# Attention scores copied by ScalarE and masked in SBUF, four banks for one set of transposes, and scratch space turned into weight buffers, in a decoder layer on one core

## The chip, the core and the metric

The kernel runs on one core of one Trainium2 chip. The time is the device time of one execution in microseconds (us), and lower is better. The core has TensorE (PE in the profile), VectorE (DVE), ScalarE (ACT), GpSimd (POOL) and SyncE (SP), each with its own instruction queue that it works through in order, and DMA queues that move data between HBM and the on-chip buffer SBUF. TensorE writes into PSUM, of which this kernel uses eight banks of 128x512 fp32 words.

## The reference, cut to what matters

One layer with two branches over the same 256 tokens: causal attention with 8 heads of 128, and a gated unit that mixes positions within chunks of 128. All matrices are fp32. With 256 tokens there is only one attention block, so the gathering of past blocks falls away and attention is causal attention over 256 keys.

```python
D_MODEL = 2048; SEQ = 256; N_ATT_HEADS = 8; HEAD_DIM = 128

h = rms_norm(x, norm_g)
q, k, v, z_a, u_b, v_b, z_b, g_a, g_b = jnp.split(h @ w_in, cuts, axis=-1)
q = rms_norm(q.reshape(B, S, N_ATT_HEADS, HEAD_DIM), q_norm_g)
k = rms_norm(k.reshape(B, S, N_ATT_HEADS, HEAD_DIM), k_norm_g)
...
s_own = jnp.where(key_pos[None, :] <= q_pos[:, None], s_own, NEG_INF)
p = jax.nn.softmax(logits, axis=-1)
...
y_a = (att * jax.nn.silu(z_a)) @ w_proj_a
sgu = spatial_gating(jax.nn.gelu(u_b), jax.nn.gelu(v_b), sgu_norm_g, w_s, b_s)
y_b = (sgu * jax.nn.silu(z_b)) @ w_proj_b
merged = jax.nn.sigmoid(g_a) * y_a + jax.nn.sigmoid(g_b) * y_b
return x + merged @ w_out
```

## The kernel before

**The stream of weights.** `schedule()` cuts all the weight matrices into 120 pieces of 128x2048 fp32 words (1 MB each), numbered 0 to 119 in the order in which they are used: 8 pieces each ("quads") for q, k, v, za, vb, ub and zb, then four times 8 quads for the gates (g) and 4 pieces of the two branch projections (proj, results `y`), then two times 8 quads for the output (out). The main loop (`for i, ... in enumerate(G)`) loads piece i+3 (`load`, SyncE's queue), prepares piece i+2 (`split`) and multiplies piece i. The number at the end of a tile's name in the tables of order below is that of its piece: `wh28` belongs to piece 28, and za's quads are 24 to 31.

**fp32 from three multiplications.** A piece arrives as `raw`. ScalarE casts it to `wh` (L125), the high half; VectorE subtracts that from `raw` and gets `wl` (L126), the low half. The activations are cut the same way (`xuh`, `xul`), and each product is three matmuls (L288). In four or five of every 8 quads, seven block products take the place of eight: VectorE first forms sums of blocks in `t` (L143, L145, L146), and both `raw` and `t` are cut, into `whp` and `wlp` (L152, L155) and `th` and `tl` (L154, L157). Such a quad costs VectorE about three times a plain one.

**Buffers.** `raw` and `t` share the tag "raw" with 4 buffers; `wh` and `th` share "wh" with 3, `wl` and `tl` share "wl" with 3; "whp" and "wlp" have 2 each. A buffer is written again only when its last reader is done: a new `wh` waits until TensorE is through with the piece three back in that tag.

**Banks.** The main loop keeps two sets of four PSUM banks, E and L, that change places with each matrix. The quads of one matrix accumulate in L, those with seven products also in E; what happens beside them (transposes, scores, attention) uses the E banks before the first such quad needs them.

**Work around the change**, hung on pieces by `at(...)`:
- after quad 24: k is transposed (`ps_kT`); after quad 25, `score` makes six tiles of scores (two groups of four heads, three blocks of 128x128 per head) in the banks E[0..3], E[0], E[1]. Two lie below the diagonal and are copied by ScalarE (L424); four lie on it and VectorE copies their allowed part over tiles that GpSimd has filled with -1e30 (L410, L411, L426). `softmax` follows: row maximum (L432), exponentials with row sums (L437), reciprocals (L440).
- after quad 32 (vb's first): the probabilities are transposed; after quad 33, `attend` multiplies them with v into the four E banks (`ps_a`), and VectorE multiplies each bank into `za` (L464). Quad 34 is the first that needs the E banks again (`seven_vb`).
- after piece 64 (the first of proj 0): `turn_z` transposes `zb` into two banks, E[2] and E[3], each used twice; ScalarE casts to `zbh` (L490), VectorE makes `zbl` (L491). Pieces 66 and 67 multiply with these.

**Order.** For the first 8 quads ScalarE's and VectorE's order is that of the code. After it a scheduler places all instructions on all engines by priorities (the order in the code) and by its own estimate of when operands will be there, TensorE's matmuls among them.

Of the kernel before, what the change touches and what calls it, by code (L numbers as in the profile page):

```python
# [12 lines left out]
F32 = mybir.dt.float32  # L13
F32R = mybir.dt.float32r
# [3 lines left out]
ALU = mybir.AluOpType  # L18
AX = mybir.AxisListType

P = 128
# [5 lines left out]
NEG_INF = -1e30  # L27
ATT_SCALE = P ** -0.5
WORDS = 2048
B = 512  # L30
# [37 lines left out]
def hybrid_layer_kernel(  # L68
# [9 lines left out]
    nc = tc.nc  # L78
# [3 lines left out]
    const = ctx.enter_context(tc.tile_pool(name="const", bufs=1))  # L82
    big = ctx.enter_context(tc.tile_pool(name="big", bufs=10))
    unit = ctx.enter_context(tc.tile_pool(name="unit", bufs=10))
    wpool = ctx.enter_context(tc.tile_pool(name="wpool", bufs=6))
# [6 lines left out]
    def u(name, dtype=F32):  # L92
        return unit.tile([P, B], dtype, tag="u", name=name)
# [9 lines left out]
    raw, wh, wl, th, tl = {}, {}, {}, {}, {}  # L103

    def strassen(i):
        if i >= NG or G[i][0] != "quad" or G[i][1] == G[0][1]:
            return False
        return G[i][3] in SK or (G[i][1] == "g" and G[i][3] == 4)
# [2 lines left out]
        nc.sync.dma_start(raw[i][:, a:b], w[i, :, a:b])  # L111

    def new_raw(i):
        raw[i] = wpool.tile([P, WORDS], F32, tag="raw", bufs=4, name=f"raw{i}")

    def load(i, pieces=1):
        if i >= NG:
# [6 lines left out]
    def halve(h, l, r):  # L124
        nc.scalar.copy(h, r)  # L125
        nc.vector.tensor_tensor(l, r, f(h), op=ALU.subtract)  # L126

    def split(i, pieces=1, js=None):
        if i >= NG:
            return  # L130
        r = raw[i]
        if not strassen(i):
            if i not in wh:
                wh[i] = wpool.tile([P, WORDS], F32R, tag="wh", bufs=3, name=f"wh{i}")
                wl[i] = wpool.tile([P, WORDS], F32R, tag="wl", bufs=3, name=f"wl{i}")
            n = WORDS // pieces
            for j in js or range(pieces):
                sl = slice(j * n, (j + 1) * n)
                halve(wh[i][:, sl], wl[i][:, sl], r[:, sl])
            return  # L140
        t = wpool.tile([P, WORDS], F32, tag="raw", bufs=4, name=f"t{i}")
        two = t[:, 0:2 * B].rearrange("p (a n) -> p a n", a=2)
        nc.vector.tensor_tensor(two, r[:, B:3 * B].rearrange("p (a n) -> p a n", a=2),  # L143
                                r[:, None, 0:B].to_broadcast([P, 2, B]), op=ALU.add)
        nc.vector.tensor_tensor(t[:, 2 * B:3 * B], t[:, 0:B], r[:, 2 * B:3 * B], op=ALU.add)  # L145
        nc.vector.tensor_tensor(t[:, 3 * B:], t[:, 2 * B:3 * B], r[:, 3 * B:], op=ALU.add)  # L146
        wh[i] = wpool.tile([P, 3 * B], F32R, tag="whp", bufs=2, name=f"whp{i}")
        wl[i] = wpool.tile([P, 3 * B], F32R, tag="wlp", bufs=2, name=f"wlp{i}")
        th[i] = wpool.tile([P, WORDS], F32R, tag="wh", bufs=3, name=f"th{i}")
        tl[i] = wpool.tile([P, WORDS], F32R, tag="wl", bufs=3, name=f"tl{i}")  # L150
        a, b = slice(0, 2 * B), slice(2 * B, WORDS)
        nc.scalar.copy(wh[i], r[:, B:])  # L152
        for sl in (a, b):
            nc.scalar.copy(th[i][:, sl], t[:, sl])  # L154
        nc.vector.tensor_tensor(wl[i], r[:, B:], f(wh[i]), op=ALU.subtract)  # L155
        for sl in (a, b):
            nc.vector.tensor_tensor(tl[i][:, sl], t[:, sl], f(th[i][:, sl]), op=ALU.subtract)  # L157

    X = {}
# [45 lines left out]
    def split_x(kp, js=None):  # L205
        i, a = kp // 4, 2 * (kp % 4)
        for j in js or range(2):
# [8 lines left out]
    make_identity(nc, ident)  # L216
    mhalf = const.tile([P, 8], F32, name="mhalf")
    nc.gpsimd.memset(mhalf, -0.5)
    tri_f = u("tri_f").rearrange("p (h t) -> p h t", t=P)
    nc.gpsimd.memset(tri_f, 1.0)  # L220
    nc.gpsimd.affine_select(out=tri_f, in_=tri_f, pattern=[[0, 4], [-1, P]], base=0,
                            channel_multiplier=1, compare_op=ALU.is_ge, fill=0.0)
    tri = const.tile([P, 4, P], U8, name="tri")
    nc.gpsimd.tensor_copy(tri, tri_f)
    gain = const.tile([P, P], F32, name="gain")
# [180 lines left out]
    def score(banks):  # L406
        X["S1"] = slot(F32, "S1").rearrange("p (h t) -> p h t", t=S)
        for hg in range(2):
            X["S0", hg] = u(f"S0{hg}").rearrange("p (h t) -> p h t", t=P)
            nc.gpsimd.memset(X["S0", hg], NEG_INF)  # L410
        nc.gpsimd.memset(X["S1"][:, :, P:], NEG_INF)  # L411
        qT, kT = X["qT"], X["kT"]
        n = 0
        for hg in range(2):
            for c, b in ((0, 0), (1, 0), (1, 1)):
                ps = bank(banks[n % 4], f"ps_s{c}{hg}{b}")
                n += 1
                for h in range(4):
                    nc.tensor.matmul(ps[:, h * P:(h + 1) * P], qT[:, 4 * hg + h, c * P:(c + 1) * P],
                                     kT[:, 4 * hg + h, b * P:(b + 1) * P], start=True, stop=True)  # L420
                pv = ps.rearrange("p (h t) -> p h t", t=P)
                dst = X["S0", hg] if c == 0 else X["S1"][:, 4 * hg:4 * hg + 4, b * P:(b + 1) * P]
                if b < c:
                    nc.scalar.copy(dst, pv)  # L424
                else:
                    nc.vector.copy_predicated(dst, tri, pv)  # L426

    def softmax(hg):
        for c in range(2):
# [21 lines left out]
    def attend(hg, banks):  # L451
        v, pt = X["v"], X["PT", hg]
        for c in range(2):
            ps = bank(banks[c], f"ps_a{hg}{c}")
            for h in range(4):
                sl = slice(h * P, (h + 1) * P)
                nc.tensor.matmul(ps[:, sl], pt[:, c, h, :], v[0][hg][:, sl], start=True, stop=(c == 0))
                if c == 1:
                    nc.tensor.matmul(ps[:, sl], pt[:, 2, h, :], v[1][hg][:, sl], start=False, stop=True)
            za = X["za"][c][hg]  # L460
            for h in range(4):
                sl = slice(h * P, (h + 1) * P)
                nc.scalar.activation(za[:, sl], za[:, sl], AF.Copy, scale=X["rc", c, hg][:, h:h + 1])
            nc.vector.tensor_tensor(za, ps, za, op=ALU.mult)  # L464

    def mix(banks):
        for c in range(2):
# [170 lines left out]
    E, L = [0, 2, 4, 3], [1, 5, 6, 7]  # L638
    e = None
    for i, (kind, name, c, kp, n) in enumerate(G):  # L640
# [8 lines left out]
        if kind == "quad":  # L649
            if n == 0:  # L650
                if i and G[i - 1][0] == "quad":

                    E, L = L, E
# [39 lines left out]
        for fn, a in later.pop(i, []):  # L693
            a = list(a)
            if fn is sums:
                a[0] = X[a[1]]
            elif a and fn in (turn_qk, score, turn_p, attend, turn_z, mix, turn_m):
                if a[-1] is None:
                    a[-1] = list(E)
                    if fn is turn_p and a[0] == 1:  # L700
                        a[-1] = [E[3], E[0], E[1]]
                    if fn is attend:
                        a[-1] = E[2 * a[0]:]
                elif a[-1] == "late":
                    a[-1] = E[2:4]
                elif a[-1] == "L01":
                    a[-1] = L[0:2]
                elif a[-1] == "L23":
                    a[-1] = L[2:4]
                elif a[-1] == "L3":  # L710
                    a[-1] = L[3:4]
            fn(*a)
# [48 lines left out]
```

## Time and profile before

| | |
|---|---|
| three runs | 665.03, 666.70 and 666.89 us, median 666.7 us |
| the profiled execution | 664.48 us, of which its span 662.8 us |
| granted TensorE clock in the span | 1.000 |
| HBM read | 132.72 MB |

The span runs from the first to the last instruction. The profile's own slices (40 equal parts of the span, the busy share in tenths, 9 is 90% or more) show what kind of kernel this is:

```profile
PE   8999999999999999999999899999999999999997
DVE  4879898999999699999999999889989989998996
ACT  7889777757895678766656745655564556746460
POOL 1003003000020004000000000000000000000000
DMA  8975544634654534745457534935573573747651
```

TensorE is busy from end to end, VectorE nearly so, ScalarE two thirds, and the DMA engines half of the time after the first 30 us. A matmul's record is longer than the distance between two matmuls (they are pipelined), so a row of nines for PE doesn't say by itself that nothing is lost: that is read from the starts.

### The profile page before, as it was taken

Reading aid. Unit: us, or ns where it says so; the run is one execution under the profiler, and the core shown is the slowest. Engines: PE = TensorE matmul, PEld = TensorE weight load, DVE = VectorE, ACT = ScalarE, POOL = GpSimd, SP = SyncE. Lnnn points to the kernel's source line nnn. Section 1 sums busy time; section 2 is a strip of 40 time slices with the busy share of each in tenths; the row PEclk is TensorE's granted clock in tenths of the full one; section 3 lists DMA queues with packets and bytes.
Section 4 is the critical chain, followed back from the end, with each engine's and each line's share of the span. In section 5 each row is a group of like instructions: output and inputs, shape, how many; then the busy total and the mean of one; then the engine's idle time right before and its main releaser. Section 6 shows DMA issues by size and latency. Waiting matters only on the chain.

```text
span 662.8 us, 7853 instructions
## 1 busy us (share of the span) xinstructions
PE 652.3 (98%) x2980; PEld 538.4 (81%) x2980; DVE 606.6 (92%) x606; ACT 427.3 (64%) x560; POOL 27.2 (4%) x28
## 2 busy tenths in 40 slices
PE   8999999999999999999999899999999999999997
PEld 4888888888888888888888788888888888888886
DVE  4879898999999699999999999889989989998996
ACT  7889777757895678766656745655564556746460
POOL 1003003000020004000000000000000000000000
PEclk9999999999999999999999999999999999999999
DMA  8975544634654534745457534935573573747651
GB/s 308 417 294 191 200 181 151 252 122 176 247 170 154 224 128 164 280 136 209 163 190 283 182 139 158 351 156 181 206 296 112 182 278 142 254 163 282 201 180 63
DMA packets 22213, 135.32 MB, mean 204 GB/s; under 512 B 2464, under 2 KB 3104, under 8 KB 7072
## 3 DMA queue, kind: packets, MB, share of 16 engines
q1 hardware_dynamic: 21024, 132.73, 54.0%
q10 hardware_dynamic: 1152, 2.10, 1.0%
q8 instruction: 23, 0.38, 0.2%
q14 instruction: 14, 0.11, 0.0%
HBM read 132.72 MB, written 2.10 MB: 203 GB/s over the span
## 4 chain that ended last, share of the span: by engine, by line
PE 83%; DVE 8%; ACT 3%; DMA 2%; issue 2%; SPq 0%; DVEq 0%; ACTq 0%
PE acc_g L288 16%; PE y L288 13%; PE acc_out L288 9%; PE seven_g L288 8%; PE acc_q L288 6%; PE acc_ub L288 5%; PE acc_zb L288 5%; PE acc_k L288 5%; PE seven_out L288 3%; PE acc_vb L288 3%; DMA raw<-in_w 2%; PE acc_v L288 2%; DVE tl L157 2%; PE seven_zb L288 2%; PE seven_ub L288 2%
## 5 line engine op out<-in xcount | busy, mean ns | idle before, releaser
L126 DVE TENSOR_TENSOR wl<-raw,wh 128x2048 fp32r<-128x2048 f32 (+2 forms) x76 | 156.2, 2063 | 29.1 <-ACT wh L125 28.9
L154 ACT CAST th<-t 128x1024 fp32r<-128x1024 f32 x104 | 108.9, 1053 | 112.5 <-DVE t L143 50.2
L125 ACT CAST wh<-raw 128x2048 fp32r<-128x2048 f32 (+2 forms) x76 | 130.9, 1730 | 51.7 <-PE acc_g L288 17.1
L157 DVE TENSOR_TENSOR tl<-t,th 128x1024 fp32r<-128x1024 f32 x104 | 126.2, 1219 | 5.0 <-ACT th L154 4.7
L152 ACT CAST whp<-raw 128x1536 fp32r<-128x1536 f32 x52 | 76.6, 1481 | 31.1 <-DMA raw<-in_w 10.7
L155 DVE TENSOR_TENSOR wlp<-raw,whp 128x1536 fp32r<-128x1536 f32 x52 | 91.1, 1752 | 2.0 <-ACT whp L152 2.0
L143 DVE TENSOR_TENSOR t<-raw 128x1024 f32<-128x1024 f32 x52 | 63.4, 1219 | 1.1 <-DMA raw<-in_w 0.8
L288 PE MATMUL acc_g<-wh,xul 128*128 128x512 f32 x96 | 37.5, 390 | 1.8 <-ACT wh L125 1.8
L288 PE MATMUL acc_g<-wl,xuh 128*128 128x512 f32 x96 | 37.3, 389 | 0.0
L288 PE MATMUL acc_g<-wh,xuh 128*128 128x512 f32 x96 | 37.3, 389 | 0.0
L145 DVE TENSOR_TENSOR t<-t,raw 128x512 f32<-128x512 f32 x52 | 36.0, 691 | 0.2
L146 DVE TENSOR_TENSOR t<-t,raw 128x512 f32<-128x512 f32 x52 | 35.9, 691 | 0.2
L288 PE MATMUL acc_q<-wh,xuh 128*128 128x512 f32 x64 | 25.2, 393 | 1.3 <-ACT wh L125 1.3
L288 PE MATMUL acc_q<-wl,xuh 128*128 128x512 f32 x64 | 25.4, 396 | 0.4 <-DVE wl L126 0.4
L288 PE MATMUL y<-wh,zbl 128*128 128x512 f32 x64 | 25.1, 392 | 0.0
L288 PE MATMUL y<-wh,zah 128*128 128x512 f32 x64 | 25.0, 391 | 0.0
L288 PE MATMUL y<-wh,zal 128*128 128x512 f32 x64 | 25.0, 390 | 0.0
L288 PE MATMUL acc_q<-wh,xul 128*128 128x512 f32 x64 | 25.0, 390 | 0.0
L288 PE MATMUL y<-wl,zbh 128*128 128x512 f32 x64 | 24.9, 390 | 0.0
L288 PE MATMUL y<-wh,zbh 128*128 128x512 f32 x64 | 24.9, 390 | 0.0
L288 PE MATMUL y<-wl,zah 128*128 128x512 f32 x64 | 24.9, 389 | 0.0
L288 PE MATMUL acc_out<-wl,mh 128*128 128x512 f32 x64 | 24.9, 389 | 0.0
(497 smaller groups left out, 1586.3 us busy)
## 6 DMA issues: line engine op xcount, KB each, us to landing
raw<-in_w SPq DMA_DIRECT2D x116, 1024.0 KB, 4.9
raw<-in_w SPq DMA_DIRECT2D x7, 512.0 KB, 8.1
xnat<-in_x SPq DMA_DIRECT2D x2, 1024.0 KB, 12.7
xres<-in_x ACTq DMA_DIRECT2D x8, 256.0 KB, 4.5
out<-out_c SPq DMA_DIRECT2D x5, 256.0 KB, 2.5
xt<-in_xT SPq DMA_DIRECT2D x2, 512.0 KB, 8.4
xt<-in_xT SPq DMA_DIRECT2D x3, 256.0 KB, 9.0
raw<-in_w SPq DMA_DIRECT2D x2, 256.0 KB, 4.2
```

The source lines that it names most:

```text
L125: nc.scalar.copy(h, r)
L126: nc.vector.tensor_tensor(l, r, f(h), op=ALU.subtract)
L143: nc.vector.tensor_tensor(two, r[:, B:3 * B].rearrange("p (a n) -> p a n", a=2), r[:, None, 0:B].to_broadcast([P, 2, B]), op=ALU.add)
L145: nc.vector.tensor_tensor(t[:, 2 * B:3 * B], t[:, 0:B], r[:, 2 * B:3 * B], op=ALU.add)
L146: nc.vector.tensor_tensor(t[:, 3 * B:], t[:, 2 * B:3 * B], r[:, 3 * B:], op=ALU.add)
L152: nc.scalar.copy(wh[i], r[:, B:])
L154: nc.scalar.copy(th[i][:, sl], t[:, sl])
L155: nc.vector.tensor_tensor(wl[i], r[:, B:], f(wh[i]), op=ALU.subtract)
L157: nc.vector.tensor_tensor(tl[i][:, sl], t[:, sl], f(th[i][:, sl]), op=ALU.subtract)
L288: nc.tensor.matmul(acc, a, b, start=(start and n == 0), stop=(stop and n == 2))
```

## The change

- **Buffers:** "raw" gets 5 buffers in place of 4, "whp" 3 in place of 2. The space is taken from `dynamic_dma_scratch_size`, set to 1024 bytes.
- **Scores:** all six tiles are copied out of PSUM by ScalarE, whole; on the four diagonal ones VectorE then writes -1e30 above the diagonal, from a one-column constant `ninf` that is read broadcast. The mask `tri` is turned round for that (strictly above the diagonal). GpSimd's three fills of the score tiles go; one small fill for `ninf` comes.
- **attend:** its multiplication by `za` is given high priority in the scheduler.
- **turn_z for zb:** four banks, E[2], E[3], L[0], L[1], each used once. L[0] and L[1] hold gate 0's accumulators until VectorE has taken them out.

```diff
-        raw[i] = wpool.tile([P, WORDS], F32, tag="raw", bufs=4, name=f"raw{i}")
+        raw[i] = wpool.tile([P, WORDS], F32, tag="raw", bufs=5, name=f"raw{i}")
...
-        t = wpool.tile([P, WORDS], F32, tag="raw", bufs=4, name=f"t{i}")
+        t = wpool.tile([P, WORDS], F32, tag="raw", bufs=5, name=f"t{i}")
...
-        wh[i] = wpool.tile([P, 3 * B], F32R, tag="whp", bufs=2, name=f"whp{i}")
+        wh[i] = wpool.tile([P, 3 * B], F32R, tag="whp", bufs=3, name=f"whp{i}")
...
+    ninf = const.tile([P, 1], F32, name="ninf")
+    nc.gpsimd.memset(ninf, NEG_INF)
...
-    nc.gpsimd.affine_select(out=tri_f, in_=tri_f, pattern=[[0, 4], [-1, P]], base=0,
-                            channel_multiplier=1, compare_op=ALU.is_ge, fill=0.0)
+    nc.gpsimd.affine_select(out=tri_f, in_=tri_f, pattern=[[0, 4], [1, P]], base=0,
+                            channel_multiplier=-1, compare_op=ALU.is_gt, fill=0.0)
...
-            nc.gpsimd.memset(X["S0", hg], NEG_INF)
-        nc.gpsimd.memset(X["S1"][:, :, P:], NEG_INF)
...
-                if b < c:
-                    nc.scalar.copy(dst, pv)
-                else:
-                    nc.vector.copy_predicated(dst, tri, pv)
+                nc.scalar.copy(dst, pv)
+                if b == c:
+                    nc.vector.copy_predicated(dst, tri, ninf[:, None, :].to_broadcast([P, 4, P]))
...
-            nc.vector.tensor_tensor(za, ps, za, op=ALU.mult)
+            with tc.high_priority():
+                nc.vector.tensor_tensor(za, ps, za, op=ALU.mult)
...
                 elif a[-1] == "late":
-                    a[-1] = E[2:4]
+                    a[-1] = E[2:4] + L[0:2]
...
-    nc = bacc.Bacc("TRN2", target_bir_lowering=False, num_devices=1)
+    nc = bacc.Bacc("TRN2", target_bir_lowering=False, num_devices=1, dynamic_dma_scratch_size=1024)
```

The scheduler's placing moves on ScalarE and VectorE from the first seven-product quad to the end, since more buffers change its estimates. Three places matter.

**ScalarE around the scores.** Before, in its order (`wh`, `whp` and `th` are casts of weights, `S` are score tiles, `sm` row sums):

```order
L154 CAST th27_1258<-t27_1252 128x1024 x2
L125 CAST wh28_1334<-raw28_1250 128x2048
L424 COPY S1_1290<-ps_s100_1302 128x4x128
L424 COPY S1_1290<-ps_s110_1320 128x4x128
L152 CAST whp29_1413<-raw29_1332 128x1536
L437 ACTIVATE S00_1291,sm_1367<-S00_1291,nm_1365 128x128 x4
```

and with the change:

```order
L154 CAST th27_1260<-t27_1254 128x1024 x2
L152 CAST whp29_1416<-raw29_1335 128x1536
L125 CAST wh28_1337<-raw28_1252 128x2048
L423 COPY S00_1293<-ps_s000_1295 128x512
L423 COPY S1_1292<-ps_s100_1302 128x4x128
L423 COPY S1_1292<-ps_s101_1308 128x4x128
L423 COPY S01_1294<-ps_s010_1315 128x512
L423 COPY S1_1292<-ps_s110_1322 128x4x128
L423 COPY S1_1292<-ps_s111_1328 128x4x128
L436 ACTIVATE S00_1293,sm_1370<-S00_1293,nm_1368 128x128 x4
L152 CAST whp30_1453<-raw30_1410 128x1536
```

The six copies stand together behind `wh28`; `whp29` has moved ahead of them, and `whp30`, which stood behind all exponentials, stands between the first four of them and the rest.

**VectorE around attend.** Before (`ps_a` are the four results of attend, `t37` and `wl36` weights of later quads):

```order
L157 TENSOR_TENSOR tl35_1676<-t35_1669,th35_1675 128x1024 x2
L143 TENSOR_TENSOR t37_1788<-raw37_1755 128x1024
L464 TENSOR_TENSOR za0_c11_1538<-ps_a00_1707,za0_c11_1538 128x512
L145 TENSOR_TENSOR t37_1788<-t37_1788,raw37_1755 128x512
L464 TENSOR_TENSOR za0_h_1539<-ps_a01_1717,za0_h_1539 128x512
L464 TENSOR_TENSOR za0_c12_1541<-ps_a10_1731,za0_c12_1541 128x512
L126 TENSOR_TENSOR wl36_1758<-raw36_1667,wh36_1757 128x2048
L464 TENSOR_TENSOR za0_c22_1540<-ps_a11_1741,za0_c22_1540 128x512
```

and with the change:

```order
L143 TENSOR_TENSOR t37_1791<-raw37_1758 128x1024
L157 TENSOR_TENSOR tl35_1679<-t35_1672,th35_1678 128x1024 x2
L145 TENSOR_TENSOR t37_1791<-t37_1791,raw37_1758 128x512
L146 TENSOR_TENSOR t37_1791<-t37_1791,raw37_1758 128x512
L464 TENSOR_TENSOR za0_c11_1541<-ps_a00_1710,za0_c11_1541 128x512
L464 TENSOR_TENSOR za0_h_1542<-ps_a01_1720,za0_h_1542 128x512
L464 TENSOR_TENSOR za0_c12_1544<-ps_a10_1734,za0_c12_1544 128x512
L126 TENSOR_TENSOR wl36_1761<-raw36_1670,wh36_1760 128x2048
L464 TENSOR_TENSOR za0_c22_1543<-ps_a11_1744,za0_c22_1543 128x512
```

`t37` is out of the way of the first three products; `wl36` still stands between the third and the fourth.

**TensorE in proj 0.** Before, in the second half of piece 65 (`ps_zb` are the second two transposes of zb):

```order
L396 MATMUL ps_zb01_3039<-ident_113,zb0_c12_2643 128x128 x4
L396 MATMUL ps_zb11_3046<-ident_113,zb0_c22_2642 128x128 x4
L288 MATMUL y0_00_2997<-wh65_2955,zah_2011 128x512
L288 MATMUL y0_00_2997<-wl65_2956,zah_2011 128x512
L288 MATMUL y0_01_2998<-wh65_2955,zal_2012 128x512
L288 MATMUL y0_01_2998<-wh65_2955,zah_2011 128x512
L288 MATMUL y0_01_2998<-wl65_2956,zah_2011 128x512
L288 MATMUL acc_g1_0_3177<-wh68_3085,xul1_101 128x512
L288 MATMUL y2_00_3089<-wh66_2993,zbl_3024 128x512
```

and with the change all four transposes stand ahead of piece 65, and its end reads:

```order
L290 MATMUL y0_01_3001<-wh65_2958,zal_2015 128x512
L290 MATMUL y0_01_3001<-wh65_2958,zah_2014 128x512
L290 MATMUL y0_01_3001<-wl65_2959,zah_2014 128x512
L290 MATMUL y2_00_3092<-wh66_2996,zbl_3027 128x512
L290 MATMUL y2_00_3092<-wh66_2996,zbh_3026 128x512
L290 MATMUL y2_00_3092<-wl66_2997,zbh_3026 128x512
```

One matmul of quad 68 (`acc_g1_0`) stood between pieces 65 and 66; it now stands with the others of quad 68, behind piece 67. On SyncE's queue the small loads for the unit (`gain`, `ws`) stand behind six and two more weight loads than before. TensorE's instructions are the same in number and kind.

## The prediction

> **What bounds the kernel now.** I read the page's busy shares, the chain of waits, the list of TensorE's waits, a table of busy time by stage, and then the timeline of each wait.
>
> ```profile
> PE 652.3 (98%) x2980; PEld 538.4 (81%) x2980; DVE 606.6 (92%) x606; ACT 427.3 (64%) x560; POOL 27.2 (4%) x28
> ...
> 427.60 21.76 PE y L288 x96
> ```
>
> The lower line is a piece of the chain of waits, with start and length in us: 96 matmuls of 512 columns in 21.76 us, so TensorE starts one every 0.227 us when nothing holds it. The change takes away no matmul, so it can win only where the starts are further apart.
>
> ```profile
> engine line waited for: us in total, times, longest us
> PE acc_g L288 <- ACT wh L125: 1.8, 1, 1.8
> PE acc_q L288 <- ACT wh L125: 1.3, 1, 1.3
> PE ps_w L203 <- DVE warm L200: 1.3, 1, 1.3
> PE ps_s L419 <- DVE S L426: 1.1, 1, 1.1
> PE seven_vb L288 <- DVE za_c L464: 0.5, 1, 0.5
> ```
>
> These are TensorE's waits. `acc_q` and `ps_w` belong to the start, whose order on ScalarE and VectorE is written by hand and where the first loads are issued as before: nothing changes there. The other three are what the change touches: the scores (`ps_s`), attend (`seven_vb`), and proj 0 (`acc_g`).
>
> ```profile
> 134.90:184.20 49.30, 48.22 (x246) 40.88 (x245) 47.85 (x54) 34.01 (x57) 0.00 (x0) 1.00 0.46 171
> 184.20:234.20 50.00, 49.50 (x254) 41.64 (x253) 43.73 (x40) 33.40 (x44) 3.64 (x2) 1.00 0.50 179
> 234.20:276.80 42.60, 42.60 (x198) 35.49 (x197) 41.66 (x48) 35.31 (x73) 8.13 (x4) 1.00 0.54 198
> 276.80:321.20 44.40, 44.40 (x214) 37.37 (x213) 43.80 (x46) 30.44 (x40) 0.00 (x0) 1.00 0.52 189
> 321.20:387.40 66.20, 64.39 (x292) 52.80 (x291) 63.79 (x63) 40.30 (x37) 0.00 (x0) 1.00 0.53 192
> ```
>
> The stages za, vb, ub, zb, and gate 0 with proj 0: length, then busy time (and number) of PE, PEld, DVE, ACT and POOL, the granted clock, and DMA. VectorE is a close second: 47.85 of 49.30 us, 41.66 of 42.60, 43.80 of 44.40. So an earlier TensorE needs VectorE to be earlier too.
>
> **The scores.**
>
> ```profile
> 147.66 3.73 PE L419 MATMUL ps_s<-kT,qT 128*128 128x128 f32 x32
> 149.36 2.42 DVE L157 TENSOR_TENSOR tl<-t,th 128x1024 fp32r<-128x1024 f32 x2
> 150.43 1.89 ACT L125 CAST wh<-raw 128x2048 fp32r<-128x2048 f32 x1
> 151.70 0.72 DVE L426 COPY_PREDICATED S<-tri,ps_s 128x512 f32<-128x512 uint8 x1
> 152.47 2.05 PE L419 MATMUL ps_s<-kT,qT 128*128 128x128 f32 x16 [1.08 <-DVE S L426]
> ...
> 367.09 0.87 PE ps_zb L396 x8
> ```
>
> Eight short matmuls take 0.87 us (last line, from the chain), 0.109 each. The first 32 fill four banks and would let the next start at 147.66 + 32 x 0.109 = 151.15; it starts at 152.47, **1.3 us** late, because VectorE is at `tl` until 151.70 and only then empties the first bank.
>
> With the change ScalarE empties it. Its six copies stand behind `wh28`, which needs the buffer that TensorE gives up with quad 25, at 147.7. In the trace this cast ran only from 150.43, since it stood behind a `th` that waited for VectorE; with a fifth `raw` buffer VectorE forms that `t` earlier.
>
> ```profile
> L424 ACT COPY S<-ps_s 128x512 f32<-128x512 f32 x2 | 1.2, 582 | 0.9 <-PE ps_s L419 0.9
> L154 ACT CAST th<-t 128x1024 fp32r<-128x1024 f32 x104 | 108.9, 1053 | 112.5 <-DVE t L143 50.2
> L152 ACT CAST whp<-raw 128x1536 fp32r<-128x1536 f32 x52 | 76.6, 1481 | 31.1 <-DMA raw<-in_w 10.7
> ```
>
> Walk ScalarE's new order with these lengths. Back from 147.66, quad 25 takes 24 x 0.227 = 5.4 us and k's 16 transposes 1.7 ahead of it, so the first of these is complete at 140.9. Four evictions like L424's end at 143.2, two `th` at 145.2, `whp29` at 146.6; `wh28` can run from 147.7 to 149.6. The first bank is then free at 150.2, 0.9 us before it is needed, the second at 150.8. I take the whole 1.3 us as gone; the bounds are 0 (`wh28` as late as in the row, copies from 152.3) and 1.3.
>
> ```profile
> L426 DVE COPY_PREDICATED S<-tri,ps_s 128x512 f32<-128x512 uint8 x4 | 2.8, 730 | 0.0
> L145 DVE TENSOR_TENSOR t<-t,raw 128x512 f32<-128x512 f32 x52 | 36.0, 691 | 0.2
> ```
>
> ScalarE gets four copies more, 4 x 0.58 = 2.3 us; it is busy 34.01 of 49.30 us in this stage, and that idle time hides them. VectorE keeps four masked copies, now with SBUF on both sides. The trace shows no such one: between 0.69 us, what 512 fp32 words take from SBUF alone (L145), and 0.73 as now, that is 0 to 0.16 us less in all. I take 0.
>
> [...]
>
> The change also adds a wait. `whp30` now stands between the first exponentials and the others, and its buffer (the third in that tag) is `whp26`'s, free when TensorE ends quad 26.
>
> ```profile
> 167.52 2.36 DVE L157 TENSOR_TENSOR tl<-t,th 128x1024 fp32r<-128x1024 f32 x2 [0.39 <-ACT th L154]
> L437 ACT ACTIVATE S<-S,nm 128x128 f32<-128x128 f32 (+1 forms) x16 | 7.0, 440 | 1.5 <-DVE nm L434 1.5
> ```
>
> Without the stall the scores end at 147.66 + 48 x 0.109 = 152.9, and quad 26 at 152.9 + 21 x 0.227 = 157.7. Behind `whp30` (1.4 us) wait twelve of the sixteen exponentials (5.6 us, counting these wider), then the two halves of `th29`, and VectorE's `tl29` waits for those: 164.7, 166.7, 168. In the trace `tl29` ended at 169.88 (the first row), 1.9 us later, while TensorE is only 1.3 us earlier. So this wait costs nothing.
>
> **Attend.**
>
> ```profile
> 200.09 1.89 ACT L125 CAST wh<-raw 128x2048 fp32r<-128x2048 f32 x1
> 203.55 2.28 DVE L126 TENSOR_TENSOR wl<-raw,wh 128x2048 fp32r<-128x2048 f32 x1
> 205.75 0.68 DVE L464 TENSOR_TENSOR za_c<-ps_a,za_c 128x512 f32<-128x512 f32 x1
> ...
> 205.59 0.39 PE L288 MATMUL seven_vb<-th,Flx 128*128 128x512 f32 x1
> 206.49 0.50 PE L288 MATMUL seven_vb<-th,Flx 128*128 128x512 f32 x1 [0.50 <-DVE za_c L464]
> ```
>
> TensorE loses 206.49 - 205.59 - 0.23 = 0.67 us, waiting for the fourth product, which stands behind `wl36`. High priority doesn't lift it over `wl36`, as the order shows; it takes `t37` (0.69, L145) out from between the others. VectorE came to `wl36` at 203.55, when `wh36` had been ready since 201.98, so the fourth product can come 0.7 to 1.6 us earlier, if ScalarE keeps pace. Against it, fourteen scalings of `za` now stand on ScalarE between the last probabilities' evictions and `wh36`, where eight stood. Bounds: 0 and 0.67 us won; I take **0.5**.
>
> **Proj 0.**
>
> ```profile
> 374.09 0.39 PE L288 MATMUL y<-wl,zah 128*128 128x512 f32 x1
> 376.29 0.50 PE L288 MATMUL acc_g<-wh,xul 128*128 128x512 f32 x1 [1.81 <-ACT wh L125]
> ...
> 374.33 1.90 ACT L125 CAST wh<-raw 128x2048 fp32r<-128x2048 f32 x1 [0.41 <-PE y L288]
> ```
>
> 376.29 - 374.09 - 0.23 = **2.0 us** lost, and it had to be lost in that order. The one matmul of quad 68 needs `wh68`; its buffer is `wh65`'s, which TensorE gives up with the last matmul of piece 65, the one just before. So ScalarE could cast only while TensorE stood still. In the new order this matmul stands behind piece 67, 48 x 0.227 = 10.9 us later. What is late next?
>
> ```profile
> 366.72 1.28 DVE L346 TENSOR_TENSOR g_c<-acc_g,g_c 128x512 f32<-128x512 f32 x2
> 371.31 1.28 DVE L491 TENSOR_TENSOR zbl<-ps_zb,zbh 128x512 fp32r<-128x512 f32 x2
> ```
>
> The two new banks are free when VectorE has read gate 0's first two accumulators, here at 367.4 and 368.0. With all transposes from 367.09 on, the third and fourth ask at 368.0 and 368.4: no stall, with 0.4 us to spare. Piece 66 starts at 367.09 + 16 x 0.109 + 24 x 0.227 = 374.3 and reads only the first two tiles of `zbl`, which were there at 372.6; with `t69` put ahead of them (1.2 us) it is 373.8. I take 2.0, with 1.0 (VectorE a us later) and 2.0 as bounds.
>
> **The buffers** cost no time of their own. What they win is seen where ScalarE waits for loads.
>
> ```profile
> 357.36 1.92 ACT L125 CAST wh<-raw 128x2048 fp32r<-128x2048 f32 x1 [2.38 <-DMA raw<-in_w]
> ```
>
> A load is issued when a buffer comes free and lands 4.9 us later (the page's median), so one buffer more starts it some us earlier. TensorE didn't wait for this cast, so I count nothing; it is the slack on which the terms above rest. GpSimd's three fills go, and nothing in TensorE's list waited for GpSimd. `gain` and `ws` come six and two loads later on SyncE's queue and are used two stages on.
>
> **The sum:** 1.3 + 0.5 + 2.0 = 3.8 us. The profiled execution took 664.48 us (span 662.8 and 1.7 around it): 660.7. The median of the runs, 666.7, lies 2.2 above that execution, so I forecast 666.7 - 3.8 = **662.9 us** for a median.
>
> **The rivals.**
>
> ```profile
> 113.13 0.39 PE L288 MATMUL seven_v<-th,Fhx 128*128 128x512 f32 x1
> 113.54 0.50 PE L288 MATMUL seven_v<-tl,Fhx 128*128 128x512 f32 x1
> ```
>
> - *All small waits go too.* Here 0.41 - 0.23 = 0.18 us is lost; I found four such places, some 0.8 us. With these and 0.2 more at attend: 4.8, 661.9 us.
> - *ScalarE takes VectorE's place at the scores.* If `wh28` ends after 150.6 the first copy ends after 151.2, and each us beyond is lost again; at the row's 152.3 all of it: 666.7 - 2.5 = 664.2. For it: the cast stands ahead of the copies, as before. Against: it waited for a `t` that comes earlier now.
> - *VectorE becomes the bound.* It is busy 98% from 234 to 321, so what is won at the scores and at attend may be lost again before 360; proj 0's 2.0 stays: 664.7. For it: the table. Against: in stage vb it is idle 6.3 of 50.0 us, where it can catch up.
> - *Slower: casts to the third `whp` buffer block ScalarE.* In most stages a `whp` cast now stands ahead of a `wh` cast (`whp35` ahead of `wh33`). Its load needs a `raw` buffer that VectorE frees with `wl31`, about 173 by my walk; it lands near 178, and ScalarE's queue stands still till then. `wl33` is made at 183.5 and TensorE asks for it at 191 (quads 31 and 32 and the transposes after 177.5). It decides where a load lands more than those 7 us later; at 0.6 us in each of ten stages it is 6.0 lost against 3.8 won: 668.9.
> - *Nothing is won:* all three waits come back as others, 666.7.
>
> **Chances.** Forecast 0.56, small waits too 0.09, ScalarE 0.10, VectorE 0.15, nothing 0.05, slower 0.05. A measurement here can tell about 0.3%, 2.0 us, from no change. The forecast, the larger gain and most of ScalarE's case lie beyond it, and under half of VectorE's: 0.78 faster, 0.17 within, 0.05 slower. The range takes the sum's bounds (4.8 to 1.0 us won, 661.9 to 665.7) and, below, the runs' own spread (665.03 is 1.7 under the median): 660.2 to 665.9.
>
> **What would show it.** Right: in TensorE's waits `ps_s` from `S` and `acc_g` from `wh` are gone; `seven_vb` is under 0.3 us; the first score copy starts before 151. Wrong: `ps_s` waits for ScalarE; TensorE waits for `wl` or `tl` between 230 and 360 (VectorE the bound); ScalarE idle ahead of `whp` for loads with TensorE waiting behind it.

## The result and the profile after

| | before | changed |
|---|---|---|
| median of 6 runs each | 666.24 us (664.47 to 666.89) | 660.78 us (660.26 to 662.89) |
| ratio | 1 | 0.993, 95% interval 0.9917 to 0.9943 |
| the profiled execution | 664.48 us, span 662.8 | 660.26 us, span 658.5 |

The changed kernel is faster by 5.5 us in the medians and by 4.2 us between the two profiled executions. The busy times on its page:

```profile
PE 650.4 (99%) x2980; PEld 538.7 (82%) x2980; DVE 606.3 (92%) x606; ACT 427.8 (65%) x564; POOL 25.3 (4%) x26
```

TensorE, VectorE and ScalarE have as much to do as before; GpSimd, without its fills, has 1.9 us less. The list of TensorE's waits (what waited for what; us in total, times, longest):

```profile
PE acc_v L290 <- DVE wl L126: 1.3, 1, 1.3
PE ps_w L203 <- DVE warm L200: 1.3, 1, 1.3
PE acc_q L290 <- ACT wh L125: 1.2, 1, 1.2
PE acc_q L290 <- DVE wl L126: 0.2, 1, 0.2
```

The three waits of the prediction (`ps_s`, `seven_vb`, `acc_g`) are gone, and one has come that it didn't see: `acc_v` waits 1.3 us for a low half. The scores in the changed kernel's timeline (start, length, engine, line, operation):

```profile
147.07 1.06 ACT L154 CAST th<-t 128x1024 fp32r<-128x1024 f32 x1 [1.78 <-DVE t L146]
148.03 1.47 ACT L152 CAST whp<-raw 128x1536 fp32r<-128x1536 f32 x1
148.50 5.52 PE L419 MATMUL ps_s<-kT,qT 128*128 128x128 f32 x48
149.40 1.90 ACT L125 CAST wh<-raw 128x2048 fp32r<-128x2048 f32 x1
151.20 2.54 ACT L423 COPY S<-ps_s 128x512 f32<-128x512 f32 x5
151.69 2.28 DVE L126 TENSOR_TENSOR wl<-raw,wh 128x2048 fp32r<-128x2048 f32 x1
153.89 2.13 DVE L425 COPY_PREDICATED_SCALAR S<-tri,ninf 128x512 f32 x3
```

All 48 score matmuls run in one piece. The first copy, though, starts at 151.20; the fifth group of matmuls asks for its bank at 148.50 + 32 x 0.109 = 151.99, so the copy (0.58) is in time by 0.2 us; the prediction's mark, a first copy before 151, is missed by as much. The new wait, in VectorE's, GpSimd's and TensorE's rows:

```profile
109.57 1.38 POOL L244 TENSOR_TENSOR rs<-ms,mhalf 128x4 f32<-128x4 f32 x1 [0.41 <-DVE ms L243]
110.98 0.23 DVE L369 TENSOR_SCALAR rs<-rs,rstd 128x4 f32<-128x4 f32 x1 [0.90 <-POOL rs L244]
111.12 0.68 DVE L146 TENSOR_TENSOR t<-t,raw 128x512 f32<-128x512 f32 x1
111.72 1.75 DVE L155 TENSOR_TENSOR wlp<-raw,whp 128x1536 fp32r<-128x1536 f32 x1
113.39 2.28 DVE L126 TENSOR_TENSOR wl<-raw,wh 128x2048 fp32r<-128x2048 f32 x1
...
114.02 0.39 PE L290 MATMUL acc_v<-wh,xuh 128*128 128x512 f32 x1
115.73 0.51 PE L290 MATMUL acc_v<-wl,xuh 128*128 128x512 f32 x1 [1.32 <-DVE wl L126]
```

VectorE waits for GpSimd's power (`pow`, in k's normalization), then finishes `t21`, makes `wlp21`, and only then `wl20`, which TensorE needs first. Before, `wl20` started at 110.07, straight behind the last of k's four small multiplies:

```profile
109.93 1.83 DVE L367 TENSOR_SCALAR rs<-rs,rstd 128x4 f32<-128x4 f32 x1 [0.75 <-POOL rs L242]
110.07 2.29 DVE L126 TENSOR_TENSOR wl<-raw,wh 128x2048 fp32r<-128x2048 f32 x1
```

So the waits for GpSimd were there before; what is new is `t21` and `wlp21` ahead of `wl20`. With a fifth `raw` buffer `t21` has somewhere to go, so the scheduler puts piece 21's sums ahead of `wl20` (e5 and e6 below bear this out). TensorE loses 115.73 - 114.02 - 0.23 = 1.48 us.

**A balance.** For every kernel I took the distances between the starts of all consecutive matmuls, less 0.227 us (0.2267 unrounded; 512 columns) or 0.109 us (128), and added up by place what is left: TensorE's lost time in us. The places are times of the profiled execution: the start, v's and k's stretch (80 to 140 us), the scores (140 to 160), the attention with its transposes (180 to 220), proj 0 (360 to 400).

| | median us | start | 80-140 | scores | attention | proj 0 | rest | behind the start |
|---|---|---|---|---|---|---|---|---|
| before | 666.24 | 4.7 | 0.35 | 1.54 | 1.32 | 2.32 | 0.76 | 6.29 |
| changed | 660.78 | 4.2 | 1.68 | 0.16 | 0.38 | 0.02 | 0.34 | 2.58 |
| e1 scores' edit alone | 666.84 | 4.9 | 0.42 | 2.09 | 1.39 | 2.15 | 0.80 | 6.85 |
| e2 banks alone | 662.58 | 5.0 | 0.25 | 1.64 | 1.35 | 0.02 | 0.75 | 4.01 |
| e3 both buffers alone | 660.57 | 5.4 | 0.60 | 0.16 | 0.39 | 0.08 | 0.36 | 1.59 |
| e4 priority alone | 665.48 | 5.4 | 0.02 | 1.64 | 1.26 | 3.94 | 0.76 | 7.62 |
| e5 `raw` buffer alone | 663.05 | 4.6 | 1.92 | 1.41 | 0.90 | 0.08 | 0.37 | 4.68 |
| e6 `whp` buffer alone | 663.43 | 4.5 | 2.73 | 1.88 | 1.31 | 0.13 | 0.77 | 6.82 |
| e7 changed, no buffers | 663.52 | 5.4 | 0.25 | 2.15 | 1.50 | 0.05 | 0.75 | 4.70 |
| e9 buffers, multiplies on GpSimd | 659.56 | 4.6 | 0.05 | 0.16 | 0.40 | 0.08 | 0.38 | 1.07 |
| e10 changed once more | 660.46 | 4.5 | 1.44 | 0.16 | 0.41 | 0.02 | 0.33 | 2.36 |
| e11 changed, multiplies on GpSimd | 659.73 | 5.9 | 0.03 | 0.16 | 0.40 | 0.02 | 0.33 | 0.94 |

The first two rows: 1.4 us came from the scores, 0.9 from the attention, 2.3 from proj 0, 0.4 from small waits and 0.5 from the start; 1.3 went to the new wait. That is 4.2, as between the profiled executions. The start differs by up to 1.7 us among kernels whose first 8 quads are the same, so its part is not the change's.

### The profile page after: what moved, and what is told of

It reads as the page before. It is cut to its first block, busy times and chain, and to the rows that moved or that the text cites. A ratio compares the mean times of both kernels' runs of the same rounds, so it can differ in the third digit from the quotient of the medians.

```text
span 658.5 us, 7820 instructions
## 1 busy us (share of the span) xinstructions
PE 650.4 (99%) x2980; PEld 538.7 (82%) x2980; DVE 606.3 (92%) x606; ACT 427.8 (65%) x564; POOL 25.3 (4%) x26
## 4 chain that ended last, share of the span: by engine, by line
PE 93%; DVE 3%; POOL 1%; DMA 1%; issue 1%; ACT 0%; SPq 0%; DVEq 0%
PE acc_g L290 16%; PE y L290 13%; PE acc_out L290 9%; PE seven_g L290 8%; PE acc_q L290 6%; PE acc_vb L290 5%; PE acc_za L290 5%; PE acc_ub L290 5%; PE acc_zb L290 5%; PE acc_k L290 4%; PE seven_out L290 3%; PE acc_v L290 2%; PE seven_vb L290 2%; PE seven_zb L290 2%; PE seven_ub L290 2%; PE seven_za L290 2%
## 5 line engine op out<-in xcount | busy, mean ns | idle before, releaser
L290 PE MATMUL acc_out<-wh,mh 128*128 128x512 f32 x64 | 24.9, 389 | 0.0
```

The costliest lines, as they stand in the source:

```text
L290: nc.tensor.matmul(acc, a, b, start=(start and n == 0), stop=(stop and n == 2))
```

## The experiments

The theory under test is the prediction's: each wait is undone by its own edit. The rival: what counts is the order that the buffers bring.

### One part of the change alone

**e1, the scores' edit alone.** The kernel before with

```diff
+    ninf = const.tile([P, 1], F32, name="ninf")
+    nc.gpsimd.memset(ninf, NEG_INF)
...
-                if b < c:
-                    nc.scalar.copy(dst, pv)
-                else:
-                    nc.vector.copy_predicated(dst, tri, pv)
+                nc.scalar.copy(dst, pv)
+                if b == c:
+                    nc.vector.copy_predicated(dst, tri, ninf[:, None, :].to_broadcast([P, 4, P]))
```

(with the turned mask, the fills left out and the smaller scratch).

> The kernel before with the scores' edit alone (copy on ScalarE, mask written in SBUF; the descriptor scratch is cut too, since the constant needs room, but no buffer is added). Theory (each wait is undone by its own edit): TensorE's 1.25 us loss at the scores goes and nothing else, so the span of 662.8 us falls by 1.1 to 1.4 us, and the losses at the attention products (0.67 us) and at the projection (1.97 us) stay. Rival (what changed is the order that the buffers bring): without the buffers ScalarE's copies come too late, the loss at the scores stays over 0.6 us and the span falls by less than 0.7 us.

Measured: 666.84 us against 665.99 us of the kernel before; ratio 1.0011, interval 0.9998 to 1.0024. Nothing is won. From e1's list of TensorE's waits, and from ScalarE's timeline:

```profile
PE ps_s L419 <- ACT S L423: 1.6, 1, 1.6
```

```profile
150.84 1.89 ACT L125 CAST wh<-raw 128x2048 fp32r<-128x2048 f32 x1
152.64 2.53 ACT L423 COPY S<-ps_s 128x512 f32<-128x512 f32 x5
```

TensorE now waits for ScalarE's copy, which stands behind `wh28`, and `wh28` is as late as it was before. The wait has changed its owner and grown from 1.25 to 1.80 us. That is the prediction's rival "ScalarE takes VectorE's place", in a kernel without the buffers. e1 also has the changed kernel's smaller scratch, and the balance shows no loss of before reduced by more than 0.2 us: the scratch by itself isn't what wins in the runs with more buffers.

**e2, the four banks alone.**

```diff
-                    a[-1] = E[2:4]
+                    a[-1] = E[2:4] + L[0:2]
```

> The kernel before with four banks for the transposes of the spatial product alone. Theory: the misplaced wait of 1.8 us for a weight half at 374 us goes, and the span falls by 1.8 to 2.2 us; the other losses stay. Rival: the loss at 374 us was the late weight half itself, which the buffers bring earlier; with the banks alone at least 1 us of it stays.

Measured: 662.58 us against 665.99; ratio 0.995, interval 0.9938 to 0.9963. All of proj 0's loss goes and nothing else; the span falls by 2.0 us, to 660.8, as the theory said. TensorE's waits of e2 that are left behind the start:

```profile
PE ps_s L419 <- DVE S L426: 1.2, 1, 1.2
PE seven_vb L288 <- DVE za_c L464: 0.6, 1, 0.6
```

The median fell by 3.4, more than the span; the last section comes back to that.

**e3, both buffers alone.**

```diff
-        raw[i] = wpool.tile([P, WORDS], F32, tag="raw", bufs=4, name=f"raw{i}")
+        raw[i] = wpool.tile([P, WORDS], F32, tag="raw", bufs=5, name=f"raw{i}")
...
-        wh[i] = wpool.tile([P, 3 * B], F32R, tag="whp", bufs=2, name=f"whp{i}")
+        wh[i] = wpool.tile([P, 3 * B], F32R, tag="whp", bufs=3, name=f"whp{i}")
```

(`t` too gets 5, and the scratch is cut).

> The kernel before with the buffers alone (five raw buffers, three for the products' high halves, scratch cut). Theory: the three named losses stay (1.25, 0.67 and 1.97 us), the new wait of 1.3 us for VectorE's low half at 114 us comes in by this edit alone, and about 1.2 us of small losses (at 12 us, 182 us, 577 us) go, so the span moves by less than 0.6 us to either side. Rival: the buffers do most of the work, the loss at 374 us falls below 1 us, and the span falls by more than 1.5 us.

Measured: 660.57 us against 665.99; ratio 0.9917, interval 0.9904 to 0.9931. This is the changed kernel's whole gain. The theory said that the span would hardly move, and fell here. The one wait of TensorE behind the start, and the scores in the timeline:

```profile
PE acc_v L288 <- DVE wl L126: 0.3, 1, 0.3
```

```profile
148.63 5.52 PE L419 MATMUL ps_s<-kT,qT 128*128 128x128 f32 x48
150.99 0.73 DVE L426 COPY_PREDICATED S<-tri,ps_s 128x512 f32<-128x512 uint8 x1
```

The wait for `wl20` comes by this edit, though shorter than in the changed kernel (the last section says why).

VectorE still empties the first bank, as before the change, at 150.99 (before: 151.70) and in time: the bank is wanted at 148.63 + 3.5 = 152.1. Here TensorE also comes later (148.63, before 147.66), since its start lost more; e9 below shows the same without that help. At the attention `wl36` starts at 202.01 (before: 203.55), the fourth product is done at 204.89, and TensorE goes on without a stop:

```profile
202.01 2.28 DVE L126 TENSOR_TENSOR wl<-raw,wh 128x2048 fp32r<-128x2048 f32 x1
204.21 0.68 DVE L464 TENSOR_TENSOR za_c<-ps_a,za_c 128x512 f32<-128x512 f32 x1
204.98 0.47 PE L288 MATMUL seven_vb<-th,Flx 128*128 128x512 f32 x1
```

**e4, the priority alone.**

```diff
-            nc.vector.tensor_tensor(za, ps, za, op=ALU.mult)
+            with tc.high_priority():
+                nc.vector.tensor_tensor(za, ps, za, op=ALU.mult)
```

> The kernel before with the priority of the attention's last multiply alone. Theory: the loss of 0.67 us at 205 us falls to about 0.1 us and the span by 0.4 to 0.7 us. Rival: the multiply waits for ScalarE's scaling of za and not for its place on VectorE, so the priority alone changes the loss by less than 0.2 us.

Measured: 665.48 us against 665.99; ratio 0.9998, interval 0.9987 to 1.001. From e4's timeline:

```profile
203.98 2.28 DVE L126 TENSOR_TENSOR wl<-raw,wh 128x2048 fp32r<-128x2048 f32 x1
206.18 0.68 DVE L465 TENSOR_TENSOR za_c<-ps_a,za_c 128x512 f32<-128x512 f32 x1
...
206.91 0.50 PE L288 MATMUL seven_vb<-th,Flx 128*128 128x512 f32 x1 [0.68 <-DVE za_c L465]
```

`wl36` stands ahead of the fourth product, and VectorE's and ScalarE's whole order is that of before, instruction by instruction. TensorE loses 0.84 us at this place instead of 0.67. The loss didn't fall, so the theory is wrong; the reason that the rival gave (ScalarE's scaling) is wrong too, since the product stands behind `wl36`.

### Which buffer

**e5, five `raw` buffers alone; e6, three `whp` buffers alone** (each with the smaller scratch).

```diff
-        raw[i] = wpool.tile([P, WORDS], F32, tag="raw", bufs=4, name=f"raw{i}")
+        raw[i] = wpool.tile([P, WORDS], F32, tag="raw", bufs=5, name=f"raw{i}")
```

> The kernel before with the fifth raw buffer alone (and the scratch cut that makes room for it). Theory (the raw buffer lets VectorE form the sums of a later piece while it would idle, so they no longer stand behind the scores and the attention): the losses at the scores and at 374 us go (under 0.3 us each), that at the attention falls, the wait for a low half at 114 us comes in, and the span ends within 1 us of that with all buffers (658.8 us). Rival (the third high-half buffer is what counts): the loss at the scores stays over 1 us and the span over 661 us.

```diff
-        wh[i] = wpool.tile([P, 3 * B], F32R, tag="whp", bufs=2, name=f"whp{i}")
+        wh[i] = wpool.tile([P, 3 * B], F32R, tag="whp", bufs=3, name=f"whp{i}")
```

> The kernel before with the third high-half buffer alone. Theory (raw buffer): the loss at the scores stays as it was (1.25 us), that at the attention does not fall (0.67 us or more), only the misplaced wait at 374 us goes, span about 660.8 us as with the banks alone, median about 662.6 us. Rival (the high-half buffer counts): all three go, span under 659.5 us.

Measured: 663.05 and 663.43 us against 665.89 us; ratios 0.9957 (0.9945 to 0.997) and 0.9965 (0.9952 to 0.9978). Both expectations failed in part: proj 0 is mended by either buffer alone, the scores by neither (1.41 and 1.88 us lost). In e5 the wait for `wl20` came as expected (0.98 us); e6, whose span I put at 660.8 us, took 663.0 in the profiled execution, the slowest of its five (the others: 661.5 to 661.8), and got a wait of its own there:

```profile
PE seven_v L288 <- DVE tl L157: 1.5, 1, 1.5
```

How far VectorE gets by the scores shows why one buffer doesn't do. The window from 30 to 148 us in the kernel before (length, then busy time of PE, PEld, DVE, ACT, POOL):

```profile
30.00:148.00 118.00, 117.98 (x539) 97.91 (x538) 105.81 (x109) 88.88 (x156) 12.98 (x12) 1.00 0.53 205
```

and with the `raw` buffer alone (e5):

```profile
30.00:148.00 118.00, 116.71 (x531) 96.43 (x530) 106.50 (x111) 89.59 (x157) 13.98 (x12) 1.00 0.59 221
```

with the `whp` buffer alone (e6):

```profile
30.00:148.00 118.00, 115.89 (x527) 95.78 (x526) 103.07 (x107) 87.95 (x155) 12.99 (x12) 1.00 0.53 204
```

and with both (e3):

```profile
30.00:148.00 118.00, 117.70 (x536) 97.62 (x536) 108.60 (x112) 91.08 (x159) 15.92 (x12) 1.00 0.59 221
```

VectorE has the same work in all four. By 148 us it has done 105.81 us of it before, 106.50 with the `raw` buffer, 103.07 with the `whp` buffer, and 108.60 with both. So with both it is 2.8 us further when the scores come; with one alone the gain is 0.7 us or none. With `raw` alone a sum can be formed early, but its casts still wait for a `whp` buffer; with `whp` alone there is no early `t` to cast: so I read it, and no run takes that apart further.

At 114 us the two runs show what each buffer moves. In e5 the last of piece 21's sums (112.64) stands ahead of `wl20` (113.24), and `wlp21` behind it (115.44). In e6 `wl20` starts at 112.21, straight behind the multiplies as before the change, and the sums follow. `t21` ahead of `wl20` is the fifth `raw` buffer's doing; `wlp21` came ahead as well only with both.

### The change without its buffers

**e7**: the changed kernel with `raw` back at 4 and `whp` at 2; scores' edit, priority and banks stay.

```diff
-        raw[i] = wpool.tile([P, WORDS], F32, tag="raw", bufs=5, name=f"raw{i}")
+        raw[i] = wpool.tile([P, WORDS], F32, tag="raw", bufs=4, name=f"raw{i}")
...
-        wh[i] = wpool.tile([P, 3 * B], F32R, tag="whp", bufs=3, name=f"whp{i}")
+        wh[i] = wpool.tile([P, 3 * B], F32R, tag="whp", bufs=2, name=f"whp{i}")
```

> The changed kernel with the buffers taken back (four raw buffers, two for the high halves); the scores' edit, the priority and the four banks stay. Theory (the buffers carry the scores and the attention, the banks only the projection): TensorE loses about 1.8 us at the scores, waiting for ScalarE's copy, and about 0.8 us at the attention, nothing at 374 us; median 662.3 to 663.3 us. Rival (the edits work together and need no buffers): median under 661.3 us.

Measured: 663.52 us against 665.89; ratio 0.9962, interval 0.9949 to 0.9976. 0.2 us over the theory's bounds and 2.2 over the rival's. The scores lose as in e1, the banks win what they win alone. TensorE's waits behind the start:

```profile
PE ps_s L419 <- ACT S L423: 1.7, 1, 1.7
...
PE ps_p L447 <- ACT PT L448: 0.4, 1, 0.4
PE seven_vb L290 <- DVE za_c L464: 0.3, 1, 0.3
```

At the attention the loss is spread over two waits now (0.53 and 0.45 us by the starts).

### The new wait

**e8 and e11**: the changed kernel with k's four small multiplies on GpSimd, behind its powers, so that VectorE waits for none of them.

```diff
-                    nc.vector.tensor_scalar(rs, rs, scale, None, op0=ALU.mult)
+                    nc.gpsimd.tensor_scalar(rs, rs, scale, None, op0=ALU.mult)
```

> The changed kernel with k's four small multiplies (rs by rstd) moved from VectorE to GpSimd, so that VectorE does not wait for GpSimd's powers ahead of the low half of piece 20. Theory: the four waits of 0.75 to 0.90 us on VectorE go, the low half is ready about 3 us sooner, the wait of 1.3 us at 114 us goes, and the span falls by 0.5 to 1.5 us (the wait takes up what the start of an execution varies by, so between executions less than 1.48 us). Rival: what stands ahead is the sums of piece 21 and not the waits, so the wait at 114 us stays over 0.8 us and the time does not change; or the longer round on GpSimd delays k's scaling and TensorE waits at k's transposes.

Measured: 659.92 us against 665.89; ratio 0.9915, interval 0.9899 to 0.9931. TensorE's wait for `acc_v` is gone. Its profiled execution was the slowest of its five (662.09 us, span 660.4) and lost 7.2 us at the start, more than any other, so its span tells nothing, and the balance has e11, the same kernel, in its place. To set it beside the changed kernel on one chip, both ran again:

> The changed kernel as it is, beside the other two on one chip. Both theories: 660.3 to 661.0 us median, the wait at 114 us there again (0.3 to 1.4 us, the longer the sooner TensorE got away at the start); it is the measure for the two others.

> The changed kernel with the four small multiplies on GpSimd once more, beside the changed kernel. Theory: 0.5 to 1.2 us faster than the changed kernel in the medians, no wait at 114 us. Rival (the difference to the changed kernel was one of two sittings): within 0.3 us of it.

Measured: 660.46 us (changed; ratio 0.9924, 0.9911 to 0.9938) and 659.73 us (e11; 0.991, 0.9894 to 0.9926) against 665.80. VectorE's and GpSimd's rows in e11's timeline:

```profile
107.65 0.69 DVE L145 TENSOR_TENSOR t<-t,raw 128x512 f32<-128x512 f32 x1
108.38 0.69 DVE L146 TENSOR_TENSOR t<-t,raw 128x512 f32<-128x512 f32 x1
108.99 1.75 DVE L155 TENSOR_TENSOR wlp<-raw,whp 128x1536 fp32r<-128x1536 f32 x1
110.66 2.28 DVE L126 TENSOR_TENSOR wl<-raw,wh 128x2048 fp32r<-128x2048 f32 x1
...
109.34 3.69 POOL L369 TENSOR_SCALAR rs<-rs,rstd 128x4 f32<-128x4 f32 x1
```

`wl20` still stands behind `t21` and `wlp21`, but nothing on VectorE waits for GpSimd, and it starts at 110.66 instead of 113.39. GpSimd's multiplies are slow (up to 3.7 us in the row, 0.23 on VectorE), and nothing waits for them.

**e9**: both buffers and these multiplies on the kernel before; the scores' edit, the priority and the banks are left out.

```diff
-        raw[i] = wpool.tile([P, WORDS], F32, tag="raw", bufs=4, name=f"raw{i}")
+        raw[i] = wpool.tile([P, WORDS], F32, tag="raw", bufs=5, name=f"raw{i}")
...
-        wh[i] = wpool.tile([P, 3 * B], F32R, tag="whp", bufs=2, name=f"whp{i}")
+        wh[i] = wpool.tile([P, 3 * B], F32R, tag="whp", bufs=3, name=f"whp{i}")
...
-                    nc.vector.tensor_scalar(rs, rs, scale, None, op0=ALU.mult)
+                    nc.gpsimd.tensor_scalar(rs, rs, scale, None, op0=ALU.mult)
```

> The kernel before with the buffers alone, and k's four small multiplies on GpSimd; the scores' edit, the priority and the four banks are left out. Theory (with both buffers the other edits are superfluous): as fast as the changed kernel with the multiplies on GpSimd, so 659.6 to 660.2 us median, no wait of TensorE over 0.3 us behind 20 us. Rival (the other edits still give some of the gain where the wait at 114 us no longer hides it): at least 0.5 us slower than the changed kernel with the same multiplies, with a wait at the scores, the attention or the projection.

Measured: 659.56 us (658.88 to 660.31) against 665.80; ratio 0.991, interval 0.9895 to 0.9924, beside the changed kernel's 660.46 us (660.30 to 661.85). The scores in e9's timeline, and all of TensorE's waits in it:

```profile
147.22 5.52 PE L419 MATMUL ps_s<-kT,qT 128*128 128x128 f32 x48
148.38 0.74 DVE L426 COPY_PREDICATED S<-tri,ps_s 128x512 f32<-128x512 uint8 x1 [0.24 <-PE ps_s L419]
```

```profile
PE ps_w L203 <- DVE warm L200: 1.3, 1, 1.3
PE acc_q L288 <- ACT wh L125: 1.1, 1, 1.1
```

Only the start is left. VectorE (110.4 us of work by 148 us, without the four multiplies) is so far ahead that it waits for the first scores (0.24 us) instead of the other way round, though TensorE comes to them earlier than before the change (147.22). With the buffers, the scores' edit, the priority and the four banks win nothing that these runs can tell. e9's and e11's medians lie 0.9 and 0.7 us under the changed kernel's, and of their ten runs only one (660.31) lies above that kernel's lowest (660.30); the intervals of the ratios still overlap.

## Why the prediction was right, and where it was not

The sign, and three named waits that would go, were right; the time, 662.9, was 2.1 us too high, inside the range. That the sum of 3.8 us came so near to the 4.2 between the profiled executions is luck in part: 1.3 us went to a wait that it didn't see, and 0.5 at the start, 0.4 of small waits, 0.4 more at attend and 0.3 more at proj 0 made up for it. By its steps:

- **Scores, 1.3 us:** right in size (1.4), wrong in what earns it. The edit was to win it because ScalarE's copy would be earlier than VectorE's. e1 and e7 show that the copy is no earlier without the buffers, and e3 that with them VectorE's is early enough. The walk itself leaned on the fifth buffer ("with a fifth `raw` buffer VectorE forms that `t` earlier"); the term belonged to that buffer and the third `whp` together. The margin was smaller than walked (0.2 us, not 0.9): `wh28` started at 149.40, not when quad 25 ended (148.50). It stood behind `whp29`, and that behind a half of `th27` that waited 1.78 us for VectorE's `t27`, a sum that the walk took as ready. In e11, where VectorE doesn't wait for GpSimd, the walk comes out: `wh28` starts at 148.49, as the scores do (148.48), the first copy at 150.30, and it ends 1.1 us before its bank is wanted.
- **The masked copies, taken as 0 with bounds up to 0.16 us less:** outside the bounds. From the changed kernel's instructions, grouped by line and shape:

```profile
L425 DVE COPY_PREDICATED_SCALAR S<-tri,ninf 128x512 f32 x4 | 2.9, 782 | 0.0
```

  782 ns each where 730 stood: 0.2 us more in all. The profile names the new form as another instruction (`COPY_PREDICATED_SCALAR` where `COPY_PREDICATED` stood), so these rows don't compare PSUM and SBUF alone. On VectorE the copying out isn't paid for, and the edit alone won nothing (e1).
- **Attend, 0.5 us:** the wait of 0.67 us went, and 0.2 us at the transposes with it. The prediction saw that priority didn't lift the product over `wl36`, yet credited the edit with taking `t37` away. e4 moves nothing; the buffers do it all.
- **Proj 0, 2.0 us:** right in size and mechanism (e2). What it missed: with either buffer more the scheduler no longer puts the one matmul of quad 68 there (e5, e6), so the edit was one of three cures.
- **The buffers, "I count nothing":** the step that failed. As "slack on which the terms above rest" they were named and priced at 0, while they carry all three terms (e3; proj 0's comes by the banks too), and they cost 1.48 us at `wl20`. That wait could be read from VectorE's order: `wl20` behind `t21`, `wlp21` and the steps that wait for GpSimd. I walked the queues only at the places of the edits.
- **From the profiled execution to the median:** the sum of 3.8 us stood against 4.2. The prediction then carried the 2.2 us by which the kernel before's median lay above its profiled execution over to the changed kernel, where it was 0.5. That made up most of the 2.1 us; the last section comes back to the 2.2.

Of the rivals, "VectorE becomes the bound" and "slower" didn't show: between 230 and 360 TensorE waits for nothing. "ScalarE takes VectorE's place" showed only without the buffers (e1, e7). "All small waits go too" came nearest in time (661.9).

## What to carry to other kernels

Where a scheduler sets the order, what a buffer costs and wins can't be read from the lines that the diff touches; walk every engine's new order, above all where a step waits for a slow engine (VectorE for GpSimd here, up to 0.90 us at a time). Before crediting an edit with a wait that goes, ask whether the engine that ended the wait has simply got ahead: how much work it has done by then tells it (105.8, 108.6 and 110.4 us here). A change of several parts is best taken apart both ways, each part alone and all without it: here the part that was to cost and win nothing did the whole work.

## What the runs showed of the hardware

**In e4 eight matmuls behind a gap of 2.19 us started 0.43 us apart.** In e4's profiled execution the misplaced matmul at proj 0 starts 2.19 us behind the one before. Right behind it, eight matmuls start 0.43 us apart instead of 0.227: 1.6 us more lost. That window of e4 (the granted clock is the number behind POOL's):

```profile
376.90:380.40 3.50, 3.50 (x9) 2.72 (x9) 3.50 (x3) 2.50 (x2) 0.00 (x0) 0.52 0.12 23
```

and the same place in the kernel before, behind as long a gap (2.20 us):

```profile
376.50:380.00 3.50, 3.50 (x16) 2.87 (x16) 3.50 (x3) 2.50 (x2) 0.00 (x0) 1.00 0.17 23
```

The clock was 0.52 in the one and 1.00 in the other, behind gaps of the same length. The slow starts of e4 take 8 x 0.43 = 3.4 us; what lowered the clock there is not shown.

The mean granted clock, which is on record for every execution, makes it likely that such stretches are common. e4's profiled execution, with one of them, has 0.997. Of the 41 executions of the kernel before that were timed beside the experiments, 22 have 0.994 to 0.997 (median 666.5 us) and 19 have 0.999 or 1.000 (median 665.1 us). Of the 51 executions of the changed kernel and of e2, e3 and e5 to e11, which have no such gap at proj 0, 7 lie under 0.999, four of them e8's. So about half of the executions of the kernel before seem to pay 1.4 us more behind this gap (666.5 - 665.1, an estimate), while its profiled one (664.48 us, clock 1.000) didn't. That would explain part of what the medians fell by beyond the traces (3.4 us against 2.0 in e2, 5.5 against 4.2 in the change). It isn't shown: only the profiled executions tell where the clock fell, and e8's three executions with 0.996 and 0.997 took 659.77 to 660.05 us, no longer than e11's, the same kernel.

**In e8 a mean clock of 0.949 left the matmuls where they were.** In e8's profiled execution the granted clock is 0.95 from 40 to 640 us, and matmuls still start 0.227 us apart. Its span is 660.4 us; the four others of e8, with clocks of 0.996 to 1.000, have spans of 657.9 to 658.3. What it lost, it lost at the start (7.2 us, against 4.2 to 5.9 in the balance).

**The wait at 114 us took up what the start lost.** The loss at 114 us was 1.48, 1.29 and 0.46 us where the start lost 4.24, 4.50 and 5.44 (changed, e10, e3): the sums are 5.7, 5.8 and 5.9. VectorE starts `wl20` at 113.39, 113.46 and 113.57 in the three, whenever TensorE got away.
